# Twenty load widths instead of eleven, and two more tiles stored in halves

## The chip, the cores and the metric

The kernel runs on one core of one Trainium2 chip. The metric is the device time of one execution in microseconds, as the median of several runs; lower is better.

## The reference

The input `x` is a float32 array of 16 batches, 8 heads, 256 query rows and 256 key columns; `lengths` holds one integer per batch. For each batch the first `length` columns of each row go through a softmax, and the columns behind them are zero in the result.

```python
for b in range(batch):
    length = lengths[b]
    masked = x[b, :, :, :length].copy()
    masked = masked - np.max(masked, axis=-1, keepdims=True)
    exp_masked = np.exp(masked)
    result[b, :, :, :length] = exp_masked / np.sum(exp_masked, axis=-1, keepdims=True)
```

The lengths are drawn once, from a fixed seed, between 128 and 255: 188, 233, 229, 243, 195, 252, 165, 210, 222, 180, 209, 157, 159, 199, 214, 248 for batches 0 to 15.

## The kernel before

**Tiles.** One batch is one tile: 2048 rows of 256 columns, 2 MB, laid out as 128 partitions with `nt` = 16 rows each. The buffer `xt` has 8 slots of one tile; the tile at position `n` lives in slot `n % 8`, and everything happens in place. There are 16 positions. `batch_of` says which batch stands at which position: positions 0, 1 and 2 take batches 1, 2 and 3, position 3 takes batch 15, position 15 takes batch 0, and positions 4 to 14 take the batch of the same number. "Tile n" below is the tile at position n.

**Loads.** Tile 0 is loaded by SP in two halves (L145). Tiles 1 to 3 are loaded in full by POOL (L196). Tiles 4 to 15 are loaded by POOL in a loop of six turns with two loads each (L205): POOL reads the batch's length into a register (L135), and `pick` (L163 to L176) searches a list of widths by comparing the length in a binary tree. Every leaf of the tree holds a load of its own with a constant width (L168) that brings only the first `w` columns of each row; rows stand 1024 bytes apart in HBM and in `xt`, so every row of a narrow load is a piece of its own of 4 × `w` bytes. The last leaf loads all 256 columns. Before the search POOL waits until the tile that had the slot, 8 positions earlier, is stored (`s_st`); at the leaf, behind the search, it waits until the load two positions earlier has landed (`s_sw`). So two loads are under way at most.

**The work on a tile.** VectorE (DVE) masks the columns from 128 on with one instruction (`mask`, `clip`, L248), which also covers old contents behind a narrow load. ScalarE (ACT) takes the exponentials: four rows at once (L374), whose sums VectorE takes (`total`, L269), then twelve rows one by one with their sums (L377). VectorE takes reciprocals (L279) and multiplies half a tile at a time (`divide`, L282). VectorE's order is written out: for each tile first half divided, next tile masked, second half divided, next tile's `total`.

**Stores.** SP issues the stores in the order of the tiles (L146 to L156), each tile in the pieces that `parts` gives (L59 to L70): tile 0 in four, tiles 1 to 7 in three (the first half, then two quarters), tiles 8 to 12 and 15 in halves, tiles 13 and 14 in one piece. A piece waits for the multiplication of the half it ends in (L149). For tiles 2 to 12 the first piece also waits until all of tile b−2 has been stored (L153). A half is 1 MB, 8 KB in each partition; a quarter is 512 KB, 4 KB in each. The last instruction waits for tile 15's store. A fallback behind the main part (L331 to L403) recomputes all in a safe way if a sum is out of range; it is not entered with this input.

Of the kernel before, what the change touches and what calls it, by code (L numbers as in the profile page):

```python
# [21 lines left out]
def kernel(  # L22
# [28 lines left out]
        return pos + 1 if pos < ahead - 1 else {ahead - 1: 15, 15: 0}.get(pos, pos)  # L51


    widths = list(range(160, 248, 8))
    low = widths[0]
    mid = seq_k // 2
    big = 1.0e30
# [1 line left out]
    def parts(b):  # L59


        if b == 0:
            cuts = [0, 2, quarter, half, nt]
        elif b < 8:
            cuts = [0, half, half + quarter, nt]
        elif b < 13 or b == batch - 1:
            cuts = [0, half, nt]
        else:
            cuts = [0, nt]
        return [slice(i, j) for i, j in zip(cuts, cuts[1:])]  # L70
# [35 lines left out]
    with tc.tile_critical(no_gpsimd_drain=True):  # L106
# [39 lines left out]
        for b in range(batch):  # L146
            s_b = s_st[b % 2] if b < late else s_late if b < batch - 1 else s_last
            for s in parts(b):
                nc.sync.wait_ge(s_out, 2 * b + (s.stop - 1) // half + 1)  # L149
                if b == 0 and s.start == 2:  # L150
                    nc.sync.wait_ge(s_min, 3)
                if 2 <= b < late and s.start == 0:
                    nc.sync.wait_ge(s_b, 64 * (b // 2 + 2))  # L153
                nc.sync.dma_start(
                    out=out_f[batch_of(b), :, s, :], in_=xt[:, b % slots, s, :]
                ).then_inc(s_b, 16 * (1 if b == 0 else (s.stop - s.start) // quarter))  # L156
# [48 lines left out]
        with nc.Fori(16, 16 * (batch // 2 - 1), 16, engines=[POOL]) as landed:  # L205
            for par in range(2):
                n = landed // 8 + (ahead - 2 + par)
                b = n % 15 if par == 1 else n
# [229 lines left out]
```

## Time and profile before

| | |
|---|---|
| median of 3 runs | 154.69 us (154.58 to 154.70) |
| span of the profiled execution, first to last instruction | 152.8 us |
| time outside the span (the median less the span; the profiled execution's own total isn't listed apart) | 1.9 us |
| VectorE busy | 134.6 us, 88% |
| ScalarE busy | 95.1 us, 62% |
| POOL busy | 21.3 us, 14% |
| DMA | 61.57 MB in 10646 packets, 403 GB/s over the span |
| HBM read, written | 27.98 MB, 33.55 MB |

The page shows the busy share of each engine in 40 slices of the span, a digit for each slice in tenths. The line "DMA" is the mean busy share of the core's 16 DMA engines. Work is attributed to a queue: q1 is the queue that SP issues on, q0 the one that POOL issues on. A packet is what a DMA engine moves before it turns to another queue. Issuing an instruction of a DMA is not counted as busy time of the engine.

### The profile page before, as it was taken

The numbers are of one execution on the slowest core, as the hardware profiler recorded it, in microseconds if no ns is written. First come the engines' busy times: TensorE is split into PE (matmuls) and PEld (weight loads), VectorE is DVE, ScalarE is ACT, GpSimd is POOL, SyncE is SP. The second block draws the span as 40 slices with busy tenths as digits, with TensorE's granted clock in tenths as the row PEclk, the third lists the DMA queues.
The fourth block names the chain that finished last, engine by engine and source line by source line (L and its number), as shares of the span: only waits on it lengthen the run. The fifth ranks groups of instructions, "written<-read, shape, count | busy, mean of one in ns | idle before, by whom it ended". The sixth has DMA issues, their size and how long they took to land.

```text
span 152.8 us, 818 instructions
## 1 busy us (share of the span) xinstructions
PE 0.3 (0%) x2; PEld 0.2 (0%) x2; DVE 134.6 (88%) x107; ACT 95.1 (62%) x402; POOL 21.3 (14%) x29
## 2 busy tenths in 40 slices
PE   0000000000000000000000000000000000000000
PEld 0000000000000000000000000000000000000000
DVE  1369999999999999999999999999999999999500
ACT  3096699339394967859393939577593939395000
POOL 4962110030303020030300220302000000000000
DMA  4999999999999999999999999999999999999994
GB/s 107 420 446 433 401 435 347 421 445 420 394 397 422 405 421 411 411 409 405 419 411 418 408 399 419 408 410 423 417 421 419 413 420 422 435 435 442 429 410 187
DMA packets 10646, 61.57 MB, mean 403 GB/s; under 512 B 898, under 2 KB 1010, under 8 KB 7058
## 3 DMA queue, kind: packets, MB, share of 16 engines
q1 hardware_dynamic: 5904, 35.65, 56.7%
q0 software_dynamic: 4736, 25.89, 41.9%
q14 instruction: 4, 0.03, 0.1%
q10 hardware_dynamic: 2, 0.00, 0.0%
HBM read 27.98 MB, written 33.55 MB: 403 GB/s over the span
## 4 chain that ended last, share of the span: by engine, by line
DVE 87%; DMA 5%; issue 1%; SPq 0%; PE 0%
DVE xt L282 48%; DVE xt L248 23%; DVE row_sum L269 12%; DMA xt<-in_x_dram 5%; DVE inv_sum L279 3%; DVE ends L317 0%; SPq L145 0%; DVE bad L320 0%; PE count L218 0%; DVE redo L328 0%; SPq L433 0%; SPq L106 0%
## 5 line engine op out<-in xcount | busy, mean ns | idle before, releaser
L377 ACT ACTIVATE xt<-xt 128x256 f32<-128x256 f32 x192 | 76.6, 400 | 0.2 <-DVE xt L248 0.2
L282 DVE TENSOR_TENSOR xt<-xt,inv_sum 128x2048 f32<-128x2048 f32 x32 | 73.3, 2292 | 1.1
L374 ACT ACTIVATE xt<-xt 128x1024 f32<-128x1024 f32 x16 | 16.9, 1056 | 42.8 <-DVE xt L248 42.8
L248 DVE SCALAR_TENSOR_TENSOR xt<-down,len_s,xt 128x2048 f32<-128x2048 f32 (+1 forms) x17 | 37.7, 2219 | 5.0 <-DMA xt<-in_x_dram 5.0
L377 ACT ACTIVATION_READ_ACCUMULATOR xt<-xt 128x1 f32 x192 | 35.9, 187 | 0.0
L168 POOL DMA_DIRECT2D xt<-in_x_dram x12 | 13.2, 1104 | 84.0 <-DMA xt<-in_x_dram 62.3
L269 DVE TENSOR_REDUCE row_sum<-xt 128x4 f32<-128x1024 f32 x16 | 19.4, 1210 | 0.0
L279 DVE RECIPROCAL inv_sum<-row_sum 128x8 f32<-128x8 f32 x32 | 6.3, 198 | 0.5
L191 POOL MEMSET xt<- 128x1536 f32 x4 | 5.4, 1398 | 1.1 <-DVE len_s L239 1.1
L361 ACT ACT_TABLE_LOAD x1 | 1.3, 1283 | 1.6 <-SPq L106 1.6
L196 POOL DMA_DIRECT2D xt<-in_x_dram x3 | 1.8, 590 | 0.0
L231 DVE TENSOR_SCALAR down<-iota_i 128x256 f32<-128x256 int32 x1 | 0.3, 300 | 1.6 <-POOL iota_i L181 1.6
L317 DVE TENSOR_REDUCE ends<-inv_sum 128x1 f32<-128x256 f32 x2 | 0.7, 408 | 0.0
L236 DVE CAST len_b<-word 1x16 bf16<-1x16 int32 x1 | 0.2, 164 | 0.4 <-DMA word<-in_lengths_dram 0.4
L239 DVE TENSOR_SCALAR len_s<-len_f 128x16 f32<-128x16 f32 x1 | 0.2, 176 | 0.3 <-PE len_f L216 0.3
L218 PE MATMUL count<-bad,ones_c 128*1 128x3 bf16 x1 | 0.2, 165 | 140.8 <-DVE bad L320 140.8
L181 POOL IOTA iota_i<- 128x256 int32 x1 | 0.3, 331 | 0.6 <-SPq L106 0.6
L328 DVE TENSOR_REDUCE redo<-count 1x1 f32<-1x3 f32 x1 | 0.1, 150 | 0.3 <-PE count L218 0.3
L320 DVE TENSOR_SCALAR bad<-ends 128x1 bf16<-128x1 f32 x3 | 0.3, 150 | 0.0
L187 POOL MEMSET seed<- 1x1 f32 x2 | 0.2, 225 | 0.0
L218 PEld LDWEIGHTS count<-bad,ones_c 128*1 128x1 bf16 x1 | 0.1, 79 | 140.8 <-DVE bad L320 140.8
L361 ACT ACTIVATE warm<-const-float32-0.0 128x1 f32<-128x1 f32 x1 | 0.2, 204 | 0.0
(10 smaller groups left out, 1.1 us busy)
## 6 DMA issues: line engine op xcount, KB each, us to landing
out_dram<-xt SPq DMA_DIRECT2D x20, 1024.0 KB
xt<-in_x_dram POOLq DMA_DIRECT2D x4, 2048.0 KB, 16.3
out_dram<-xt SPq DMA_DIRECT2D x15, 512.0 KB
xt<-in_x_dram POOLq DMA_DIRECT2D x3, 1728.0 KB, 16.7
out_dram<-xt SPq DMA_DIRECT2D x2, 2048.0 KB
xt<-in_x_dram POOLq DMA_DIRECT2D x2, 1600.0 KB, 16.0
xt<-in_x_dram POOLq DMA_DIRECT2D x2, 1280.0 KB, 14.7
xt<-in_x_dram SPq DMA_DIRECT2D x2, 1024.0 KB, 6.4
```

The source lines that it names most:

```text
L168: nc.gpsimd.dma_start(out=xt[:, slot, :, :w], in_=x_n[:, b, :, :w]).then_inc(s_sw[par], 16)
L191: nc.gpsimd.memset(xt[:, b, :, low:], 0.0).then_inc(s_fill, 1)
L196: nc.gpsimd.dma_start(out=xt[:, b], in_=x_f[batch_of(b)]).then_inc(s_sw[b - 1] if b < 3 else s_ld[2], 16)
L218: nc.tensor.matmul(count, lhsT=ones_c, rhs=bad, start=True, stop=True).then_inc(s_count, 1)
L248: return nc.vector.scalar_tensor_tensor(out=t, in0=down[:, None, lo:hi].to_broadcast([P, s.stop - s.start, hi - lo]), scalar=len_s[:, batc ...
L269: nc.vector.tensor_reduce(out=row_sum[:, b % slots, :lump], in_=xt[:, b % slots, :lump, :], op=ALU.add, axis=AX,).then_inc(s_exp[0], 1)
L279: step(nc.vector.reciprocal(out=inv_sum[:, b, s], in_=row_sum[:, b % slots, s]))
L282: nc.vector.tensor_tensor(out=t, in0=t, in1=inv_sum[:, b, s, None].to_broadcast([P, half, seq_k]), op=ALU.mult,).then_inc(s_out, 1)
L317: step(nc.vector.tensor_reduce(out=ends[:, k : k + 1], in_=values, op=op, axis=AX))
L361: nc.scalar.activation(out=warm, in_=nc.const_aps.tensor(0.0, (P, 1), F32), func=EXP)
L374: nc.scalar.activation(out=e, in_=e, func=EXP).then_inc(s_lump, 1)
L377: ins = nc.scalar.activation(out=e, in_=e, func=EXP, accum_out=row_sum[:, slot, j : j + 1])
```

## The change

Two constants change. The list of widths for narrow loads was 160, 168, ..., 240 and becomes 160, 164, ..., 236; the search tree then has 21 leaves instead of 12, and a length of 237 to 240 would go to the full load. Tiles 6 and 7 are stored in two halves, where they were stored in a half and two quarters. Nothing changes for VectorE, ScalarE and TensorE.

```diff
-    widths = list(range(160, 248, 8))
+    widths = list(range(160, 240, 4))
...
         if b == 0:
             cuts = [0, 2, quarter, half, nt]
-        elif b < 8:
+        elif b < 6:
             cuts = [0, half, half + quarter, nt]
         elif b < 13 or b == batch - 1:
             cuts = [0, half, nt]
```

For the drawn lengths the width picked by the narrow loads is, by position:

| position | 4 | 5 | 6 | 7 | 8 | 9 | 10 | 11 | 12 | 13 | 14 | 15 |
|---|---|---|---|---|---|---|---|---|---|---|---|---|
| length | 195 | 252 | 165 | 210 | 222 | 180 | 209 | 157 | 159 | 199 | 214 | 188 |
| before | 200 | 256 | 168 | 216 | 224 | 184 | 216 | 160 | 160 | 200 | 216 | 192 |
| after | 196 | 256 | 168 | 212 | 224 | 180 | 212 | 160 | 160 | 200 | 216 | 188 |

## The prediction

> **What bounds the kernel now.** I read four views: the page for who is busy, the chain of waits for what VectorE does last, the stretches of the end for what happens after that, and the DMA view stretch by stretch for what the traffic costs. The page first: tenths of busy time in 40 slices, then the two big DMA queues (packets, MB, share of 16 engines).
>
> ```profile
> DVE  1369999999999999999999999999999999999500
> ...
> DMA  4999999999999999999999999999999999999994
> ...
> q1 hardware_dynamic: 5904, 35.65, 56.7%
> q0 software_dynamic: 4736, 25.89, 41.9%
> ...
> HBM read 27.98 MB, written 33.55 MB: 403 GB/s over the span
> ```
>
> Two resources are full at once, VectorE and the DMA engines. q1 carries the stores (and the first 2 MB of loads), q0 the other loads. Which of the two sets the end is told by the end of the chain (start, duration, what) and by the stretches behind it (length, busy time of PE, PEld, DVE, ACT, POOL, clock, DMA share, GB/s).
>
> ```profile
> 131.61 2.26 DVE xt L248
> ...
> 136.31 1.14 DVE row_sum L269
> ...
> 140.15 2.29 DVE xt L282
> 142.44 0.74 DVE ends L317 x3
> ```
>
> ```profile
> 126.80:142.40 15.60, 0.00 (x0) 0.00 (x0) 15.39 (x13) 10.41 (x49) 0.00 (x0) 1.00 1.02 432
> 142.40:151.30 8.90, 0.17 (x1) 0.08 (x1) 1.20 (x8) 0.00 (x0) 0.00 (x0) 1.00 0.93 396
> 151.30:152.80 1.50, 0.00 (x0) 0.00 (x0) 0.00 (x0) 0.00 (x0) 0.00 (x0) 1.00 0.00 0
> ```
>
> VectorE finishes the last result at 142.44, yet the DMA engines work on until 151.3 and move 8.9 us × 396 GB/s = 3.5 MB after it. Only 1 MB of that is the result just finished; the rest is backlog. From 126.8 on there are only stores, at 432 GB/s, so the last 1.05 MB takes 2.43 us and its turn comes at 148.9, over 6 us after its data are ready. The DMA engines set the end. A microsecond of DMA work taken away anywhere comes off the end, as long as the engines never run dry; a microsecond of VectorE time costs nothing until the backlog is used up. The backlog is smallest for tile 14: its 2 MB store takes 4.85 us and stands in front of tile 15's two halves, so its turn comes at 151.3 − 2×2.43 − 4.85 = 141.6; its data are ready at 136.31. With some 1.5 us for the store to be issued and to begin (my estimate, from the 1.5 us that lie between 151.3 and the span's end, the nearest row that shows a transfer's handshake), 3.8 us of cover are left there.
>
> The runs have a median of 154.69 us, the profiled span is 152.8; 1.9 us lie outside the first and last instruction and stay. I apply the changes to the span one to one and give the result on the median. Differences under 0.2%, 0.31 us, are what a measurement of this kernel can't tell from no change.
>
> **Stores of tiles 6 and 7.** When do they move? SP issues tile b's store when tile b−2's has landed, so the store rows of SP's timeline give the times (start, length, line, count).
>
> ```profile
> 84.74 1.55 SPq L154 DMA_DIRECT2D out_dram<-xt  x3
> ...
> 94.28 0.89 SPq L154 DMA_DIRECT2D out_dram<-xt  x2
> ...
> 104.03 0.91 SPq L154 DMA_DIRECT2D out_dram<-xt  x2
> ```
>
> The three pieces at 84.74 are tile 7's, issued on the landing of tile 5; the pairs at 94.28 and 104.03 are tiles 8 and 9, on the landing of 6 and 7. So tiles 6 and 7 move from 84.3 to 103.5, and from 103.5 on every store is in halves, which is what 6 and 7 become. The DMA view of 84.3 to 103.5 and then of 103.6 to 123.1:
>
> ```profile
> DMA packets 1720, 7.87 MB, mean 410 GB/s; under 512 B 129, under 2 KB 165, under 8 KB 1465
> q1 hardware_dynamic: 862, 4.19, 53.6%
> q0 software_dynamic: 858, 3.68, 48.3%
> ...
> DMA packets 1420, 8.14 MB, mean 417 GB/s; under 512 B 106, under 2 KB 116, under 8 KB 789
> q1 hardware_dynamic: 709, 5.17, 63.7%
> q0 software_dynamic: 711, 2.97, 38.0%
> ```
>
> Store cost per MB, in engine time: first stretch 0.536 × 16 × 19.2 us = 164.7 us for 4.19 MB, 39.3 us per MB; second stretch 0.637 × 16 × 19.5 = 198.7 us for 5.17 MB, 38.4 per MB. A quarter piece moves 4 KB per partition, a half 8 KB, and the larger packets pay the fixed part half as often. The two tiles' 4.19 MB save 4.19 × 0.88 = 3.7 us of engine time, over 16 engines 0.23 us. The shares add up to 1.02, so in time it is 0.22 us. It comes off the end: **−0.22**.
>
> What else moves: packets of the two queues alternate (709 against 711, 862 against 858), so larger store packets leave loads less. Loads got 3.68 MB in 19.2 us, 192 GB/s; in halves 2.97 in 19.5, 152 GB/s. Over the 19.2 us loads lose 0.76 MB, which at 152 GB/s makes them 5.0 us later. That is covered, but narrowly: the last load's row, and the time of its issue (the last of the 12 moves), are
>
> ```profile
> xt<-in_x_dram POOLq DMA_DIRECT2D x1, 1536.0 KB, 21.0
> ...
> L168 POOLq MOVE xt<-in_x_dram x12: 29/29/38, 13.9 to 105.6; - x12
> L173 POOLq COMPARE_BRANCH  x47: 34/40/55, 11.1 to 105.3; - x47
> ...
> POOL xt L168 <- DMA xt<-in_x_dram: 62.3, 9, 12.9
> ```
>
> Tile 15 lands at 105.6 + 21.0 = 126.6, VectorE wants it at 131.61: 5.0 us of slack, about all used. If it is a little late, VectorE waits, and behind that stand the 3.8 us of cover at tile 14's store. So the delay costs nothing up to 8.8 us. In return the stores run 3 us ahead of today, and the backlog at the end is the same total.
>
> **Narrow loads.** Only positions 4 to 15 pick a width. By the drawn lengths five of these twelve change, each by 4 columns, 16 bytes a row: positions 4, 7, 9, 10 and 15 (200→196, 216→212, 184→180, 216→212, 192→188). No length lies between 237 and 240, where the new list would load the full 256. That is 5 × 2048 rows × 16 B = 0.164 MB, or 5 × 128 = 640 rows on each DMA engine. What 16 bytes of a row cost I take from two loads of neighbouring widths: position 14 (216 columns, rows of 864 B) is moving in 105.2 to 116, position 15 (192 columns, 768 B) in 117 to 126.
>
> ```profile
> q0 software_dynamic: 397, 1.64, 37.8%
> ...
> q0 software_dynamic: 312, 1.39, 38.7%
> ```
>
> 0.378 × 16 × 10.8 us / (1.64 MB / 864 B) = 34.4 ns a row; 0.387 × 16 × 9 us / (1.39 MB / 768 B) = 30.8 ns. Three steps of 32 B cost 3.6 ns, 1.2 ns a step. Every row in this trace is a whole number of such steps, so what half a step saves is not shown. In proportion it saves 0.6 ns a row: 640 × 0.6 = 0.40 us with rounding. If a row with a broken end costs like the next whole step, it saves nothing. If the broken end costs a step more, it loses 640 × 1.2 = 0.77 us. I take **0**: rows stand 1024 B apart in both memories, so the 16 bytes at a row's end have no neighbour that could share their step, and the nearest priced row above, which is today's, is the better guide. Both ends are kept for the range.
>
> [...]
>
> **POOL's search.** The tree has 21 leaves instead of 12. For the drawn lengths the twelve searches take 52 comparisons instead of 44, at 40 ns: 0.3 us in all, 0.03 us a load. The search is done before the wait for the load two places earlier, on which POOL idles 62.3 us in nine waits, so this costs nothing; were that cover gone, it would delay each load by 0.03 us and fall under the 5 us slack. SP issues two stores fewer and waits just as often.
>
> Sum: −0.22 + 0 + 0 → 154.47.
>
> **The rivals.**
> 1. *The bytes count in proportion.* −0.22 − 0.40 → 154.07, faster by 0.4%. For it: cost per byte hardly depends on width (34.4/864 and 30.8/768 are both 0.040 ns). Against it: all of that was seen in whole steps.
> 2. *A broken row end costs a step more* (the other side). −0.22 + 0.77 → 155.24, slower. Its place is q0 in the five loads; it decides from 0.53/640 = 0.83 ns a row upwards. For it: nothing in the trace bounds such an end, as none occurs. Against it: only that the fixed costs seen are small.
> 3. *Loads too late*, also slower: if tile 15 comes over 8.8 us late instead of 5.0, the end moves one to one, at 10 us by 1.2 us, to 155.7. It needs a further delay of 3.8 us at POOL. One mechanism: its loop is longer, and if its code must be fetched anew on each turn, each fetch goes through the same full DMA engines. Against it: POOL idles 62.3 us, and one load is always in flight when it issues the next. [...]
> 4. *The store term doesn't come*: halves cost less only because of what loads ran beside them. 154.69, no change.
>
> **How the numbers follow.** Chances: forecast 0.50, rival 1 0.17, rival 2 0.18, rival 3 0.08, rival 4 0.07. Around each I allow 0.15 us for the rounding of the shares and for run to run. The bound on the fast side is 154.69 − 0.31 = 154.38, 0.09 below my forecast, so about a quarter of the forecast's chance falls past it: faster 0.50 × 0.27 + 0.17 × 0.95 ≈ 0.30. Slower: 0.18 × 0.85 + 0.08 × 0.9 + 0.03 for the tails ≈ 0.25. Within 0.2%: 0.45. The range reaches from rival 1 less its 0.15 (153.9) to rival 2 plus 0.26 (155.5), leaving out the far part of rival 3.
>
> **What would show it.** In the profile after: q1 with 512 packets fewer of 4 KB and 256 more of 8 KB, so about 5616 in all (two stores' 32 completion packets fewer), and HBM read 27.98 − 0.16 = 27.82 MB. Tile 9's stores issued near 101 instead of 104.03. q0's share × span, now 64.0 us, unchanged by the forecast, 63.6 by rival 1, 64.8 by rival 2. Tile 15 landing near 131, a small or no new wait of VectorE at L248 late in the span. DMA tenths of 9 to the end. The prediction is wrong if VectorE's last result comes more than 4 us later, if the DMA line has holes, or if q0's time rises.

## The result: slower by 0.4%, and the profile after

The changed kernel took 155.26 us in the median (154.92 to 155.85) beside 154.60 us before, on the same chip. The ratio is 1.0039 with a 95% interval of 1.0026 to 1.0052: slower, by 0.6 us. The forecast was a gain of 0.2 us, so the sign was wrong, although the time lies in the range.

The page of the changed kernel:

```profile
span 153.6 us, 825 instructions
...
DMA  4999999999999999999999999999999999999992
...
q1 hardware_dynamic: 5616, 35.65, 56.7%
q0 software_dynamic: 4736, 25.72, 41.6%
q14 instruction: 5, 0.04, 0.1%
...
HBM read 27.82 MB, written 33.55 MB: 400 GB/s over the span
```

The packets and bytes are what the change says: q1 has 5616 packets, HBM reads 27.82 MB, and the packets under 512 B fall from 898 to 866, the 32 of two stores. The DMA line is full to its last digit, which is lower than before. q0's engine time is 0.416 × 153.6 = 63.9 us (64.0 before), q1's 0.567 × 153.6 = 87.1 us (86.6 before). Less traffic, the same work for the engines, and still a later end. Where is the 0.8 us of span? Nearly all of it lies in the last 2.5 us before the last store has landed. Two stretches of before, then two of after, each ending with the last landing, with the DMA share and the GB/s at the end of the row:

```profile
148.80:151.30 2.50, 0.00 (x0) 0.00 (x0) 0.00 (x0) 0.00 (x0) 0.00 (x0) 1.00 0.78 328
150.30:151.30 1.00, 0.00 (x0) 0.00 (x0) 0.00 (x0) 0.00 (x0) 0.00 (x0) 1.00 0.45 188
```

```profile
149.60:152.10 2.50, 0.00 (x0) 0.00 (x0) 0.00 (x0) 0.00 (x0) 0.00 (x0) 1.00 0.51 216
151.10:152.10 1.00, 0.00 (x0) 0.00 (x0) 0.00 (x0) 0.00 (x0) 0.00 (x0) 1.00 0.12 49
```

Before, the engines are busy 78% of that time, after only 51%: (0.78 − 0.51) × 2.5 = 0.7 us per engine is idle time, while the store as a whole isn't finished. In the last microsecond 188 KB begin to move before, 49 KB after, which is six packets of 8 KB for 16 engines. The mean time of an engine has hardly changed (150.7 us for q0 and q1 before, 151.0 after), but the engines now finish further apart: 1.0 us and 0.4 us before the stores' last packet ends, 14 and 9 of their packets are under way in the trace of before, 6 and 1 in that of after. The end of the stores waits for the last ones.

There is one more thing in the page that the forecast had no term for, the queue q14, which carries instructions. Before:

```profile
q14 instruction: 4, 0.03, 0.1%
```

Four packets became five, 0.03 MB became 0.04, each packet 8 KB and 309 to 312 ns in the two traces. One of the five lies in 12 to 17 us, where the kernel before has none; both have two in 17 to 30 us and two in 60 to 70:

```profile
q14 instruction: 1, 0.01, 0.4%
```

0.4% of 16 engines × 5 us is 0.32 us of engine time for that packet, 309 ns by its record.

VectorE is late, as the forecast allowed. First the end of its chain, then the issue of the last load and its landing:

```profile
134.20 2.35 DVE xt L248
...
142.83 2.29 DVE xt L282
145.12 0.74 DVE ends L317 x3
```

```profile
L168 POOLq MOVE xt<-in_x_dram x12: 29/29/38, 14.9 to 112.3; - x12
```

```profile
xt<-in_x_dram POOLq DMA_DIRECT2D x1, 1504.0 KB, 21.3
```

By the sum that the prediction used, tile 15 lands at 112.3 + 21.3 = 133.6 (126.6 before). VectorE masks it at 134.20 instead of 131.61, and its last result comes at 145.1 instead of 142.4. The end of the stores is not moved by that: 2.7 us is less than the 3.8 us of cover, and the run with the 20 widths alone, which comes next, has the same loss with that mask at 131.88.

### The profile page after: what moved, and what is told of

Same layout as the page of the kernel before. It is cut to its first block, busy times and chain, and to the rows that moved or that the text cites. A ratio compares the mean times of both kernels' runs of the same rounds, so it can differ in the third digit from the quotient of the medians.

```text
span 153.6 us, 825 instructions
## 1 busy us (share of the span) xinstructions
PE 0.3 (0%) x2; PEld 0.2 (0%) x2; DVE 134.9 (88%) x107; ACT 95.0 (62%) x402; POOL 21.3 (14%) x29
## 3 DMA queue, kind: packets, MB, share of 16 engines
q1 hardware_dynamic: 5616, 35.65, 56.7%
HBM read 27.82 MB, written 33.55 MB: 400 GB/s over the span
## 4 chain that ended last, share of the span: by engine, by line
DMA 82%; DVE 8%; issue 3%; POOL 1%; POOLq 1%; PE 0%; ACTq 0%; SPq 0%
DMA xt<-in_x_dram 81%; DVE xt L282 4%; DVE xt L248 2%; POOL xt L191 1%; DMA word<-in_lengths_dram 1%; DVE row_sum L269 1%; POOLq L168 1%; DVE ends L317 0%; POOL xt L196 0%; DVE inv_sum L279 0%; DVE bad L320 0%; DVE len_s L239 0%; PE len_f L216 0%; PE count L218 0%; DVE len_b L236 0%
```

## The experiments

Three theories were set against each other: **A**, the longer search code costs time, because code is fetched over the same DMA engines (q14 above); **B**, rows that end inside a step of 32 bytes, eight columns, cost time; **C**, the halves of tiles 6 and 7 cost it, through later loads. The first four kernels each take one part.

**The 20 widths alone.**

```diff
-    widths = list(range(160, 248, 8))
+    widths = list(range(160, 240, 4))
```

> The 20 widths with the old stores. The trace of the changed kernel shows the five narrower loads costing a DMA engine as much as before, the total of busy DMA time unchanged, and a longer tail in which only some DMA engines still work. Theory A (the longer search code: more code is fetched over the DMA engines, one engine falls behind and ends last): all of the loss is here, +0.6 us on the kernel before, some 155.2, with one more code packet in the instruction queue. Theory B (broken row ends cost time): also +0.6. Theory C (the halves of tiles 6 and 7 cost the time, by later loads): no loss here, 154.6.

Measured: 155.18 us, ratio 1.0040 (1.0025 to 1.0055). The whole loss is here, and so is the tail: the last 2.5 us have a DMA share of 0.54.

**The halves alone.**

```diff
-        elif b < 8:
+        elif b < 6:
```

> Tiles 6 and 7 in halves with the old 11 widths. Theory C (halves): +0.6 us, some 155.2, the last load landing at about 133 and VectorE late by 2 to 3 us at tile 15. Theories A and B: no loss, and a gain of up to 0.2 us from the larger packets, 154.4 to 154.6, though the last load lands as late as in the changed kernel.

Measured: 154.61 us beside 154.58, ratio 1.0008 (0.9991 to 1.0025). No loss: theory C is out. The last load is late here too, issued at 110.3 instead of 105.6, and it costs nothing. Nor is there the gain of 0.2 us, which lies outside the interval (0.14 us faster to 0.39 us slower); its last 2.5 us look like those of before:

```profile
148.70:151.20 2.50, 0.00 (x0) 0.00 (x0) 0.00 (x0) 0.00 (x0) 0.00 (x0) 1.00 0.76 321
```

**The long tree with the old bytes.** The tree has 21 leaves, and each leaf loads a width rounded up to a multiple of 8.

```diff
-    widths = list(range(160, 248, 8))
+    widths = list(range(160, 240, 4))
...
-                w = ws[0]
+                w = (ws[0] + 7) // 8 * 8
```

> The search tree of 21 leaves, but each leaf loads its width rounded up to the next multiple of 8, so that the loads move what they moved before; old stores. Theory A (longer code): +0.6 us, 155.2. Theory B (broken row ends): no change, 154.6. Theory C: no change.

Measured: 154.84 us, ratio 1.0015 (1.0006 to 1.0023). Code alone costs 0.26 us, clear of zero and less than half of the loss. The instruction queue has its fifth packet, 0.04 MB, and the tail resembles that of the changed kernel, with the same work for the engines as before:

```profile
149.30:151.80 2.50, 0.00 (x0) 0.00 (x0) 0.00 (x0) 0.00 (x0) 0.00 (x0) 1.00 0.57 239
```

**The short tree with the new bytes.** Twelve leaves, with the widths that the drawn lengths pick in the changed kernel.

```diff
-    widths = list(range(160, 248, 8))
+    widths = [160, 168, 180, 188, 196, 200, 212, 216, 224, 232, 240]
```

> A tree of 12 leaves as before, whose list holds the widths that the drawn lengths pick in the changed kernel (160, 168, 180, 188, 196, 200, 212, 216, 224, 232, 240), so that the loads move the bytes of the changed kernel with code of the old length; old stores. Theory A: no change, 154.6. Theory B: +0.6 us, 155.2. Theory C: no change.

Measured: 154.78 us, ratio 1.0017 (1.0004 to 1.0031), 0.2 us with an interval that nearly reaches zero. Neither A nor B has it all, and their sum, 0.46 us, falls a little short of 0.6. Moving 0.164 MB less gains nothing at any rate.

**A row's end, at a larger dose.** Three kernels have the old tree and the old stores, but let all eleven narrow loads bring 4, 8 or 1 columns more, so that 1408 rows on each engine grow instead of 640 shrinking.

```diff
-                w = ws[0]
+                w = ws[0] + 4 if ws[0] < seq_k else seq_k
```

> The old tree and stores, but each of the eleven narrow loads brings 4 columns more than its leaf's width, so that all eleven have rows that end 16 bytes past a whole 32. Compared with the next kernel, which brings 8 more. If a broken row end takes a whole step and nothing beside it, both give the same time: 1408 rows on each DMA engine at 1.2 ns, +1.7 us on the kernel before, 156.3. If the broken end itself costs time beyond the step, as 0.2 us for the five broken loads of the run with the short tree suggests, this one is 0.44 us slower than the next (11/5 of 0.2). If half a step costs half, this one is 0.85 us faster than the next.

> Each of the eleven narrow loads brings 8 columns more, a whole step of 32 bytes: +1.7 us on the kernel before by the price of a step from the profile before, some 156.3. It is the partner of the run with 4 columns more.

> Old tree and stores; each of the eleven narrow loads brings 1 column more, 4 bytes a row. If any fraction of a 32-byte step is charged as a whole step, it takes what 4 and 8 columns more took, 156.9 to 157.1. If the time goes with the bytes, it takes an eighth of the 2.6 us that 8 columns took, 154.9.

Measured: 156.92 us with 4 columns more (ratio 1.0170, 1.0147 to 1.0193), 157.11 with 8 (1.0177, 1.0154 to 1.0199), 157.18 with 1 (1.0169, 1.0156 to 1.0182). Four bytes more in a row cost as much as 32: 2.63 us for 4 bytes, 2.40 for 16, 2.59 for 32, each beside the kernel before. So in these loads a fraction of a step is charged as a whole one, and no cost of a broken end beyond that is seen. The effect of 11/5 of 0.2 us, 0.44 us, that the run before suggested did not show: the kernels with broken ends are 0.2 us below and 0.1 us above the whole step, each interval being 0.2 to 0.35 us wide on either side. A whole step costs 2.6 us / 1408 = 1.8 ns a row, not the 1.2 ns that I had read from two loads. How the charge is made can be seen in the shares of q1 and q0, with 4 columns more, 8 and 1:

```profile
q1 hardware_dynamic: 5904, 35.65, 56.3%
q0 software_dynamic: 4784, 26.25, 42.3%
```

```profile
q1 hardware_dynamic: 5904, 35.65, 56.0%
q0 software_dynamic: 4912, 26.61, 42.5%
```

```profile
q1 hardware_dynamic: 5904, 35.65, 56.5%
q0 software_dynamic: 4736, 25.98, 42.1%
```

Times their spans of 155.2, 155.4 and 155.7 us, q0 takes 65.6, 66.0 and 65.5 us, and q1 87.4, 87.0 and 88.0. Beside the whole step, broken ends leave the loads' own packets a little shorter, but the stores that run beside them get longer by as much or more: the sums are 153.0, 153.1 and 153.5 us, against 150.7 before. Whoever looks at q0 alone sees a saving that isn't there.

**How the cost grows with the code.** Trees of 8, 16, 18 and 42 leaves, all moving the bytes of the kernel before, with the old stores. The edit is that of 42 leaves. The trees of 16 and 18 have the eleven old widths and four or six between them, rounded up in the same way; the tree of 8 has only the seven widths that the lengths pick.

```diff
-    widths = list(range(160, 248, 8))
+    widths = list(range(160, 242, 2))
...
-                w = ws[0]
+                w = (ws[0] + 7) // 8 * 8
```

> A tree of 8 leaves with the seven widths that the drawn lengths pick in the kernel before, and 256: the same bytes, shorter code; old stores. If code packets count, it has as many as the kernel before or fewer: 154.6 with four, 154.3 with three. If only the search counts, no change.

> A tree of 16 leaves that moves the bytes of the kernel before; old stores. If the loss of the longer tree comes with the fifth code packet, then the time is 154.5 to 154.6 where the instruction queue shows four such packets and 154.8 where it shows five, with nothing between. If the loss grows with the number of comparisons or leaves, 154.65.

> A tree of 18 leaves, as the one of 16. By packets: 154.5 to 154.6 with four, 154.8 with five. By the number of leaves: 154.7.

> A tree of 42 leaves, each loading its width rounded up to a multiple of 8, so the bytes of the kernel before; old stores. If code packets on the DMA engines are what the longer tree costs, then this tree, more than three times as long as the old one, brings several more code packets (over 5) and a longer tail, and is slower than the tree of 21 leaves: 155.1 to 156. If the cost of that tree was the comparisons or chance, it stays at 154.6 to 154.9.

| leaves | median, us | ratio to before | instruction queue, MB | DMA share, last 2.5 us | last 1.0 us |
|---|---|---|---|---|---|
| 8 | 154.56 | 1.0009 (0.9992 to 1.0027) | 0.03 | 0.77 | 0.41 |
| 12 (before) | 154.5 to 154.6 | | 0.03 | 0.78 | 0.45 |
| 16 | 155.04 | 1.0032 (1.0020 to 1.0044) | 0.03 | 0.61 | 0.14 |
| 18 | 154.85 | 1.0020 (1.0003 to 1.0036) | 0.04 | 0.75 | 0.43 |
| 21 | 154.84 | 1.0015 (1.0006 to 1.0023) | 0.04 | 0.57 | 0.12 |
| 42 | 172.41 | 1.1147 (1.1132 to 1.1163) | 0.26 | 0.07 | 0.06 |

The shares are those of one profiled execution each. (The tree of 8 leaves lists five packets, but 0.03 MB as before: the fifth carries next to nothing.)

The cost is no straight line. Below 12 leaves nothing is won, between 16 and 21 it is 0.3 to 0.5 us, at 42 it is 17.9 us. At 42 leaves much more happens. The page, the waits, and the last microsecond before the last store has landed:

```profile
DMA  4999999999999989999899999979799999984990
...
q14 instruction: 32, 0.26, 0.4%
```

```profile
POOL xt L168 <- issue: 47.9, 5, 10.8
DVE xt L248 <- DMA xt<-in_x_dram: 23.8, 8, 4.9
```

```profile
168.00:169.00 1.00, 0.00 (x0) 0.00 (x0) 0.00 (x0) 0.00 (x0) 0.00 (x0) 1.00 0.06 25
```

Code comes in 32 packets instead of 4, 30 of them between 20 and 140 us, while the loop runs. POOL waits 47.9 us for nothing that the profile shows (15.5 before), its loads come late, VectorE waits 23.8 us for them (5.0 before), and now the DMA line has holes. I read this as the mechanism of rival 3: code of the loop is fetched anew on its way, through DMA engines that are full. Which code a packet brings, and what POOL waits for in the 47.9 us, is not shown. The last row shows one thing more. A share of 0.06 is what one engine of 16 amounts to: for a whole microsecond, in which 25 KB begin to move, the end waits for one engine's worth of work.

My expectation that the loss of the small trees comes exactly with the fifth packet did not hold: the tree of 16 leaves has 0.03 MB within its span and loses the most. The DMA share of its last microsecond is 0.14, and another part of its loss lies behind the last store, in the closing of the program, where SP waits longer for the other engines (1.0 us in two waits at L433; 0.6 before). From 151 to 156 us its instruction queue has two packets where the kernel before has one; whether that second packet causes the wait isn't shown. The tree of 18 leaves, the other way round, has the fifth packet and no thin last microsecond; in its profile the engines idle earlier, with shares of 0.98 and 0.97 in 5 to 10 and 10 to 15 us (1.04 and 1.02 before). The end of the stores of the tree of 16 leaves:

```profile
149.10:151.60 2.50, 0.00 (x0) 0.00 (x0) 0.00 (x0) 0.00 (x0) 0.00 (x0) 1.00 0.61 256
```

**Code without search.** Is it the length of the code, or the deeper search? Here the tree keeps its 12 leaves, and 45 or 90 memsets of one element each, into a tile that nobody reads, stand on POOL ahead of the loop or behind it. POOL runs them while it would wait, or after its last load.

```diff
         nc.gpsimd.wait_ge(s_fill, slots - ahead)
+        for i in range(90):
+            nc.gpsimd.memset(pad[:, i : i + 1], 0.0)
```

> The kernel before with 90 tiny memsets (one element each, of a tile nobody reads) on POOL between its fills and the loop: the tree keeps 12 leaves and its search, but the loop's code stands 90 instructions later, so that it ends about where that of the 21-leaf tree ends. They run in time in which POOL waits for the first load to land. If code length and its fetching are what the longer tree costs: +0.25 to +0.5 us, 154.8 to 155.0, with a fifth code packet or a low DMA share in the last 2.5 us. If the search or the 21 leaves themselves cost it: no change, 154.6.

> The same with 45 memsets, where the loop's code ends about where that of the tree of 16 leaves ends. Code theory: 154.8 to 155.0. Search theory: 154.6.

> The same 90 memsets behind the loop, where POOL runs them after its last load: the program is as long as in the first of the three, but the loop stands where it stood. If the loop's place in the code counts: 154.6. If the whole length of POOL's program counts, however it is used: 154.8 to 155.0.

Measured beside 154.59 us: 155.00 us with 90 ahead (ratio 1.0019, 1.0002 to 1.0037), 154.79 with 45 ahead (1.0008, 0.9990 to 1.0025), 154.95 with 90 behind (1.0009, 0.9988 to 1.0029). The medians are 0.2 to 0.4 us up in all three; only the first interval excludes zero. Five of the 29 runs of the kernel before took 155.2 to 155.6 us, which raises its mean and leaves its median; all 12 runs with 45 ahead, all 11 with 90 behind and 11 of the 12 with 90 ahead lie above that median. In all three the instruction queue shows five packets, and the last 2.5 us have a DMA share of 0.53, 0.55 and 0.62 (the last 1.0 us 0.10, 0.13 and 0.14). For 90 ahead:

```profile
149.30:151.80 2.50, 0.00 (x0) 0.00 (x0) 0.00 (x0) 0.00 (x0) 0.00 (x0) 1.00 0.53 223
```

So POOL's program need not search longer to leave this tail; in these profiles it is enough that it is longer, wherever the added part stands. The last of the five packets comes before 70 us with 90 ahead, in 149 to 152 us with 45 ahead and in 110 to 114 with 90 behind, and the tail is much the same.

**The change with a short tree.** Tiles 6 and 7 in halves and the new bytes, with 12 leaves.

```diff
-    widths = list(range(160, 248, 8))
+    widths = [160, 168, 180, 188, 196, 200, 212, 216, 224, 232, 240]
...
-        elif b < 8:
+        elif b < 6:
```

> The changed kernel with a tree of 12 leaves: tiles 6 and 7 in halves, the same narrow loads as in the changed kernel, code of the old length. If code is the larger part of the loss, it is 0.3 us or more below the changed kernel's 155.2: 154.6 to 154.8. If code and row ends are a chance split and the loss hangs on something else in the change, it stays at 155.2.

Measured: 154.71 us, ratio 1.0013 (1.0000 to 1.0025). It differs from the changed kernel in the tree alone, and of the 0.6 us some 0.15 is left. Its last microsecond has a share of 0.24. No version tried is faster than the kernel before beyond its interval.

## Why the prediction was wrong, point by point

**POOL's search: the step that failed.** "So this costs nothing" priced the added comparisons, 0.03 us a load, and left out the added code. The comparisons may well cost nothing: the memsets add none and leave much the same tail, a share of 0.53 to 0.62 in the last 2.5 us (0.51 in the changed kernel). The code costs 0.26 us with the old bytes, and taking it out of the full change brings the median from 155.26 to 154.71, most of the loss. Rival 3 named code that is fetched anew, but as harmless up to a further delay of 3.8 us at POOL, because I looked for its effect at the loads. At 21 leaves the loss appears in another place, at the end of the stores; at 42 leaves the loads do come late, as in rival 3, VectorE waits 23.8 us for them, and the kernel is 17.9 us slower. None of the three signs of being wrong that I had named came: VectorE's last result is 2.7 us later, the DMA line has no holes, and q0's time did not rise. None of them looks at the last microseconds.

**"A microsecond of DMA work taken away anywhere comes off the end."** It did not hold for the mean over 16 engines. The sum of q0 and q1 is 150.7 us before and 151.0 after; the end moved by 0.8 us, and 0.7 us of that is idle time while the last store finishes. What sets the end is the packets that finish last: 1.0 us ahead of it 14 were under way before, 6 after. The row that should have warned me was in my own fence: in 142.4 to 151.3 the DMA share was 0.93 where it had been 1.02, so some engine time was idle ahead of the end.

**The stores of tiles 6 and 7.** The timing was right: tile 9's stores were issued at 100.75 ("near 101"). The engine time was right as well. From 84.2 to 100.2, while the two tiles were stored, the DMA view of the changed kernel has

```profile
q1 hardware_dynamic: 573, 4.18, 63.0%
```

which is 0.630 × 16 × 16.0 / 4.18 = 38.6 us per MB, against 39.3 before and 38.4 forecast. In the trace of before a store packet of 4 KB took 163 ns and one of 8 KB 315 ns in 84.3 to 103.5: two of 4 KB cost 12 ns more than one of 8. What failed is the transfer of this 0.2 us to the end: with the halves alone the time did not change (interval 0.9991 to 1.0025). Rival 4 has the time of that run but not its reason: summed over all records of the two traces, q1 takes 86.73 us before and 86.55 with the halves alone, so the saving is there.

**Narrow loads.** Zero gain was right, and so was the case behind it, that a row with a broken end costs like the next whole step: with 1, 4 and 8 columns more the times were 157.18, 156.92 and 157.11 us. That it is so because rows stand 1024 B apart, as I argued, is not shown. Rival 1 is out. Rival 2 has the sign of the result but not its mechanism: a broken end costs no step more. The term for a whole step was too small, 1.8 ns a row instead of 1.2. I had priced it on the load queue alone: with 8 columns more q0 grows by 2.0 us, 1.4 ns a row, and q1, the stores beside, by 0.4 us. The run with the short tree did lose 0.2 us with the new widths; where that comes from stays open, as 11 loads with broken ends showed no such cost.

**Late loads.** The delay was forecast as 5.0 us and came out as 7.0 (126.6 to 133.6). With the halves alone the last load is issued 4.7 us later, so the forecast of that step was good; with the 20 widths alone it is issued at 107.1, 1.5 us later, which the forecast did not have. The cover held, both in the changed kernel and with the halves alone.

**What stays open.** First, what is shown: the longer tree costs most of the 0.6 us, and in the last microsecond the DMA share is 0.06 to 0.14 in every kernel with longer code on POOL but the tree of 18 leaves, and 0.24 to 0.45 in the kernels with code of the old length or less. Longer code costs 0.3 to 0.5 us by the trees of 16 to 21 leaves; the memsets, whose medians are 0.2 to 0.4 us up, say that the search is not needed for it, by one interval out of three. How the longer code brings the engines apart is not shown. The records do not name the engine of a packet, so that an added code packet of 0.32 us puts its engine behind until the end is an inference. Against a simple count stand the tree of 16 leaves, which has the thin tail without it, and that of 18, which has it without the tail.

## What to carry to other kernels

When the DMA engines are full to the end, look at the DMA share of the last few microseconds before trusting a sum of bytes or of engine time: here the engine time of q0 and q1 grew by 0.3 us and the span by 0.8, of which 0.7 were idle time in the last 2.5 us. A table of variants that was unrolled into code wasn't free here just because its comparisons were hidden behind waits: 0.3 to 0.5 us with 16 to 21 leaves, 17.9 us with 42. Count its instructions and look at the instruction queue in the profile, above all inside a loop. Cutting rows by less than a whole 32-byte step moved 0.164 MB less here and gained no time (154.78 us beside 154.58).

## What was not expected of the hardware

A program that is longer by 90 one-element memsets on an engine that is idle 86% of the time took 0.3 to 0.4 us more, by the ratio and by the medians, with the memsets ahead of the loop, and a tree of 42 leaves in place of 12 cost 17.9 us. Loads whose rows end 4 bytes past a step made the stores beside them longer, q1 from 86.6 to 88.0 us of engine time with 1 column more (87.0 with a whole step), so that here the price of a load's shape was partly paid in another queue.
